# Feed-forward in eleven joint gate-and-up groups of 512 columns, with the product split on VectorE and its tiles 128 bytes further on

## The chip, the core and the metric

One core of a Trainium2 chip runs the whole kernel. The metric is device time in microseconds of one execution. TensorE (PE, with its weight loads as PEld), VectorE (DVE), ScalarE (ACT), GpSimd (POOL) and the DMA queue of SyncE (SP) each work through a list of instructions in order and wait for one another by semaphores.

## The reference

Two layers of a sequence encoder over 256 positions of 2048 features, in float32. Each layer projects x, runs three groups of attention heads, projects back, and ends with a gated feed-forward part, which is what the change touches:

```python
D_FF = (8 * D_MODEL + 3 * 256 - 1) // (3 * 256) * 256      # 5632
...
for li in range(DEPTH):
    ...
    x = layer_norm(DEEPNORM_ALPHA * x + mix, ln1_g[li], ln1_b[li])
    ffn = (jax.nn.silu(x @ w_gate[li]) * (x @ w_up[li])) @ w_down[li]
    x = layer_norm(DEEPNORM_ALPHA * x + ffn, ln2_g[li], ln2_b[li])
```

## The kernel before

**Number format.** Every float32 operand of a large product is cut into a rounded part and a rest (names in `h` and `l`: `whi` and `wlo` for weights, `xth` and `xtl` for the transposed activations, `gth` and `gtl` for the transposed gated product). Each product is three matmuls: hi by hi, lo by hi, hi by lo. The activations (128 features by 128 positions) are the stationary operand, and the weights, up to 512 columns, are the moving one.

**Groups and steps.** `run_groups` takes all products of the kernel as one list of groups. A group has up to 1024 weight columns in two blocks, and `nk` steps of 128 weight rows. In each step and for each half `t` of the positions TensorE does three matmuls on each of the two blocks. So a group of 16 steps is 192 matmuls and a down-projection of 22 steps 264. The four sums (2 halves by 2 blocks) lie in PSUM banks, of which the pool `mm` has five, so the next group starts in the spare bank and then needs the banks of the last one in the order in which they are evacuated. In the last step TensorE finishes the banks one by one, half 0 block 0 first, and each is evacuated as it ends.

**Weights.** `load_pair` brings two steps of weight rows by DMA into one of three `raw` buffers. `convert` makes `whi` on ScalarE (L224) and `wlo` on VectorE (L225), up to four steps ahead, into six buffers.

**Feed-forward.** `ffn_groups` cuts the 5632 inner columns in two halves of 2816. A half is three pairs of groups of 1024, 1024 and 768 columns, first a gate group, then an up group; a group of 768 has two blocks of 384. The gate group's banks leave through a Silu on ScalarE (L1038) into a tile `sil` (four buffers); the up group's banks are multiplied with it on VectorE (L1042). Two down-projection groups (1024 of the 2048 output columns each) end the half. I call the gate and up groups the *ff* stage and the others the *dn* stage; over both layers there are four of each.

**Between the two.** Each product block of 512 columns is handed to a task, `t_g`: sixteen VectorE transposes per block into `gtr` (L406, four at a time), then a rounded copy to `gth` on ScalarE (L285) and the rest to `gtl` on VectorE (L286). Tasks are dealt out between the matmuls in program order by a budget: 0.65 for a step and half at 1024 columns, less for narrower groups. The numbers that tasks yield are this planner's costs. So the pieces of `t_g` stand on ScalarE between the weight conversions, and the Silu of a gate group stands behind whatever pieces were dealt out before it.

**Addresses.** In the built program `raw`, `whi`, `wlo`, `xth` and `xtl` all begin at byte addresses that are 32 modulo 256 within a partition. `gth` begins at 149408 and `gtl` at 171936, which are 160 modulo 256.

Of the kernel before, what the change touches and what calls it, by code (L numbers as in the profile page):

```python
# [10 lines left out]
F32 = mybir.dt.float32  # L11
F32R = mybir.dt.float32r
BF16 = mybir.dt.bfloat16
AF = mybir.ActivationFunctionType
ALU = mybir.AluOpType
AX = mybir.AxisListType

P = 128
SEQ = 256
# [3 lines left out]
KD = D // P  # L23
# [6 lines left out]
OFF_C = OFF_B + 3 * B_W  # L30
OFF_G = OFF_C + 4 * C_W
D_FF = 5632
HALF_FF = D_FF // 2
KH = HALF_FF // P
REL = 513
CHUNK = 64
ALPHA = (2.0 * DEPTH) ** 0.25
# [6 lines left out]
SKEW = 3  # L44
PIECES = ((0, 2), (2, 4), (4, 8), (8, 12), (12, 16))
FAR_AHEAD = 4
EVAC_ACT = (0, 1)
LAST_SKEW = 6
WARM = 9
MM_BUFS = 5  # L50
AUX_BUFS = 3
# [83 lines left out]
class Trunk:  # L135
# [18 lines left out]
    def setup(self):  # L154
# [14 lines left out]
        wps = self.aux()  # L169
        for i in range(WARM):  # L170
            nc.tensor.matmul(wps, warm[:, 0:P], warm, start=True, stop=True)
# [843 lines left out]
    def ffn_groups(self, l):  # L1015
        groups = []
        box = {}
        widths = [1024, 1024, 768]
        for hf in range(2):
            c = 0  # L1020
            for wi, w in enumerate(widths):
                bw = w // 2
                blocks = [(0, bw), (bw, bw)]
                col0 = hf * HALF_FF + c
                kt0 = c // P
                for gu in range(2):
                    def src(k, gu=gu, col0=col0, w=w):
                        return [(self.rows(self.w_up if gu else self.w_gate, l, k * P, col0, w), 0, w)]

                    def start(hf=hf, wi=wi, gu=gu):  # L1030
                        if wi == 0 and gu == 0:
                            self.gt = [self.gpool.tile([P, KH, SEQ], F32R, name=n, tag=n) for n in ("gth", "gtl")]

                    def evac(t, b, bank, gu=gu, bw=bw, kt0=kt0, hf=hf):
                        nc = self.nc
                        if gu == 0:
                            s = self.gpool.tile([P, 512], F32, name="sil", tag="sil", bufs=4)
                            nc.scalar.activation(out=s[:, 0:bw], in_=bank[:, 0:bw], func=AF.Silu)  # L1038
                            box["s", t, b] = s
                        else:  # L1040
                            g = box["s", t, b]
                            nc.vector.tensor_tensor(out=g[:, 0:bw], in0=bank[:, 0:bw], in1=g[:, 0:bw], op=ALU.mult)  # L1042
                            self.tasks.add(self.t_g(g, bw, kt0 + b * bw // P, t, hf))

                    first = hf == 0 and wi == 0 and gu == 0
                    g = dict(name=f"ff{l}.{hf}.{wi}.{gu}", nk=KD, width=w, blocks=blocks, src=src, start=start,
                             evac=evac, lhs=self.hooks_lhs, skew_in=SKEW if first else 1)
                    if first:
                        g["after"] = self.hooks_after
                    groups.append(g)  # L1050
                c += w
            for gi in range(2):
                last = hf == 1 and gi == 1

                def src(k, gi=gi, hf=hf):
                    return [(self.rows(self.w_down, l, hf * HALF_FF + k * P, gi * 1024, 1024), 0, 1024)]

                def lhs(k, t, hf=hf):
                    self.tasks.force(lambda: ("g", hf, k, t) in self.flags)
                    s = slice(t * P, (t + 1) * P)  # L1060
                    return self.gt[0][:, k, s], self.gt[1][:, k, s]

                def start(hf=hf, gi=gi):
                    if hf == 1 and gi == 0:
                        box["stats"] = self.ln_stats()
                        self.ln_load(self.ln2_g, self.ln2_b, l)

                def evac(t, b, bank, hf=hf, gi=gi, last=last):
                    self.res_evac(t, 2 * gi + b, bank, hf == 0, box["stats"] if hf else None)
                    if last and b == 1:  # L1070
                        self.ln_ready(t, box["stats"])
                        if l == DEPTH - 1:
                            for i, (k0, k1) in enumerate(PIECES):
                                self.hooks["apply"](t, i)
                                s = slice(k0 * P, k1 * P)
                                self.nc.sync.dma_start(out=self.out[0, t * P:(t + 1) * P, s], in_=self.xs[t][:, s])

                groups.append(dict(name=f"dn{l}.{hf}.{gi}", nk=KH, width=1024, blocks=[(0, 512), (512, 512)], src=src,
                                   lhs=lhs, start=start, evac=evac))
                if last:  # L1080
                    groups[-1]["skew_out"] = SKEW if l < DEPTH - 1 else LAST_SKEW
                    if l < DEPTH - 1:
                        groups[-1]["mid"] = lambda: self.hooks["need"](0, 0)
        return groups

    def t_g(self, g, bw, kt, t, hf):
        nc = self.nc
        n = bw // P
        gt = self.gpool.tile([P, 4, P], F32, name="gtr", tag="gtr", bufs=2)
        gv = g.rearrange("p (k c) -> p k c", c=P)  # L1090
        yield 1, 0.0
        yield from self.dve_tr(gt, gv, n)
        s = slice(t * P, (t + 1) * P)
        self.split(gt[:, 0:n], self.gt[0][:, kt:kt + n, s], self.gt[1][:, kt:kt + n, s])
        for i in range(n):
            self.flags.add(("g", hf, kt + i, t))
        yield 1, 0.6

    def run(self):
        self.setup()  # L1100
# [31 lines left out]
```

## Time and profile before

| | |
|---|---|
| median of 3 runs | 2394.16 us (2393.36 to 2395.81) |
| the profiled execution, its own time | 2394.55 us |
| its span, first to last instruction | 2392.8 us |
| mean granted TensorE clock | 0.992 |
| TensorE busy | 2350.1 us |
| VectorE busy | 1500.5 us |
| ScalarE busy | 1053.2 us |
| read from HBM | 437.25 MB, 184 GB/s over the span |

The profiled execution's time is 1.75 us more than its span and 0.39 us more than the median. Busy time is the time in which an engine had an instruction in work. Matmuls overlap, so the length of one matmul in the profile is not the time that it costs: what counts is how far apart the starts are, which is the length of a full stretch divided by its number of matmuls.

### The profile page before, as it was taken

Reading aid. Unit: us, or ns where it says so; the run is one execution under the profiler, and the core shown is the slowest. Engines: PE = TensorE matmul, PEld = TensorE weight load, DVE = VectorE, ACT = ScalarE, POOL = GpSimd, SP = SyncE. Lnnn points to the kernel's source line nnn. Section 1 sums busy time; section 2 is a strip of 40 time slices with the busy share of each in tenths; the row PEclk is TensorE's granted clock in tenths of the full one; section 3 lists DMA queues with packets and bytes.
Section 4 is the critical chain, followed back from the end, with each engine's and each line's share of the span. In section 5 each row is a group of like instructions: output and inputs, shape, how many; then the busy total and the mean of one; then the engine's idle time right before and its main releaser. Section 6 shows DMA issues by size and latency. Waiting matters only on the chain.

```text
span 2392.8 us, 28220 instructions
## 1 busy us (share of the span) xinstructions
PE 2350.1 (98%) x10922; PEld 1968.1 (82%) x10922; DVE 1500.5 (63%) x2420; ACT 1053.2 (44%) x1387; POOL 54.9 (2%) x120
## 2 busy tenths in 40 slices
PE   9999999999999999999999999999999999999998
PEld 7887788888888888888788877888888988889886
DVE  5755555758766448667577454557577754487675
ACT  5646454444343344343345554544443343443432
POOL 0001100000000000000000020000000000000000
PEclk9999999999999999999999999999999999999999
DMA  8654455655466555565556544566555565555653
GB/s 279 207 181 158 141 171 199 211 194 194 145 195 206 189 193 183 166 186 193 179 180 206 192 146 140 175 210 211 179 197 151 189 205 190 193 193 150 202 193 106
DMA packets 135414, 441.17 MB, mean 184 GB/s; under 512 B 12560, under 2 KB 19696, under 8 KB 134256
## 3 DMA queue, kind: packets, MB, share of 16 engines
q1 hardware_dynamic: 135136, 439.31, 56.5%
q8 instruction: 85, 1.39, 0.2%
q14 instruction: 49, 0.40, 0.0%
q10 hardware_dynamic: 144, 0.07, 0.0%
HBM read 437.25 MB, written 2.10 MB: 184 GB/s over the span
## 4 chain that ended last, share of the span: by engine, by line
PE 81%; DVE 13%; issue 2%; ACT 1%; DMA 1%; POOL 1%; SPq 0%; POOLq 0%; ACTq 0%
PE mm L272 77%; DVE gtr L406 6%; DVE wlo L225 4%; DMA raw<-w_up 1%; PE aux L295 1%; ACT whi L224 1%; PE aux L542 1%; DVE gtl L286 1%; DVE sil L1042 1%; PE aux L414 1%; DVE x L340 0%; POOL mixc L609 0%; PE aux L715 0%; PE aux L625 0%; DVE bst L319 0%
## 5 line engine op out<-in xcount | busy, mean ns | idle before, releaser
L225 DVE TENSOR_TENSOR wlo<-raw,whi 128x1024 fp32r<-128x1024 f32 (+3 forms) x849 | 991.4, 1173 | 745.2 <-ACT whi L224 739.9
L224 ACT CAST whi<-raw 128x1024 fp32r<-128x1024 f32 (+3 forms) x849 | 849.9, 1010 | 1011.8 <-PE mm L272 979.1
L272 PE MATMUL mm<-whi,xth 128*128 128x512 f32 (+2 forms) x2688 | 831.4, 384 | 23.7 <-ACT sil L1038 23.1
L272 PE MATMUL mm<-wlo,xth 128*128 128x512 f32 (+2 forms) x2688 | 815.9, 379 | 0.0
L272 PE MATMUL mm<-whi,xtl 128*128 128x512 f32 (+2 forms) x2688 | 814.9, 378 | 0.0
L272 PEld LDWEIGHTS mm<-whi,xth 128*128 128x128 f32 x2688 | 491.3, 189 | 107.8 <-ACT sil L1038 26.7
L272 PEld LDWEIGHTS mm<-whi,xtl 128*128 128x128 f32 x2688 | 500.5, 189 | 85.3 <-DVE xtl L286 0.6
L272 PEld LDWEIGHTS mm<-wlo,xth 128*128 128x128 f32 x2688 | 500.8, 189 | 83.8
L406 DVE STREAM_TRANSPOSE gtr<-sil 32x128 f32<-32x128 f32 (+1 forms) x768 | 223.9, 292 | 12.0
L272 PE MATMUL mm<-whi,gth 128*128 128x512 f32 x704 | 226.0, 395 | 0.0
L272 PE MATMUL mm<-whi,gtl 128*128 128x512 f32 x704 | 226.0, 395 | 0.0
L272 PE MATMUL mm<-wlo,gth 128*128 128x512 f32 x704 | 225.9, 395 | 0.0
L272 PEld LDWEIGHTS mm<-whi,gtl 128*128 128x128 f32 x704 | 132.6, 188 | 31.1
L272 PEld LDWEIGHTS mm<-wlo,gth 128*128 128x128 f32 x704 | 132.6, 188 | 31.0
L272 PEld LDWEIGHTS mm<-whi,gth 128*128 128x128 f32 x704 | 132.5, 188 | 30.7
L285 ACT CAST gth<-gtr 128x512 fp32r<-128x512 f32 (+1 forms) x48 | 28.1, 586 | 205.2 <-DVE gtr L406 205.2
L329 POOL TENSOR_SCALAR ve<-mv 128x1 f32<-128x1 f32 x8 | 4.7, 591 | 1809.4 <-DVE mv L327 1809.3
L285 ACT CAST xth<-aux 128x512 fp32r<-128x512 f32 (+1 forms) x58 | 28.9, 512 | 29.5 <-PE aux L295 26.0
L286 DVE TENSOR_TENSOR xtl<-aux,xth 128x512 fp32r<-128x512 f32 (+1 forms) x58 | 33.6, 592 | 5.1 <-ACT xth L285 4.8
L1042 DVE TENSOR_TENSOR sil<-mm,sil 128x512 f32<-128x512 f32 (+1 forms) x48 | 29.1, 643 | 11.8 <-PE mm L272 11.8
L286 DVE TENSOR_TENSOR gtl<-gtr,gth 128x512 fp32r<-128x512 f32 (+1 forms) x48 | 30.7, 639 | 0.1
L340 DVE SCALAR_TENSOR_TENSOR x<-x,rs,lnb 128x512 f32<-128x512 f32 (+1 forms) x40 | 24.7, 639 | 2.8 <-POOL rs L331 2.7
(154 smaller groups left out, 683.9 us busy)
## 6 DMA issues: line engine op xcount, KB each, us to landing
raw<-w_down SPq DMA_DIRECT2D x88, 1024.0 KB, 5.2
raw<-w_in SPq DMA_DIRECT2D x78, 1024.0 KB, 4.9
raw<-w_gate SPq DMA_DIRECT2D x64, 1024.0 KB, 5.0
raw<-w_up SPq DMA_DIRECT2D x64, 1024.0 KB, 5.1
raw<-w_out SPq DMA_DIRECT2D x32, 1024.0 KB, 5.2
raw<-w_in SPq DMA_DIRECT2D x52, 512.0 KB, 3.9
raw<-w_gate SPq DMA_DIRECT2D x32, 768.0 KB, 4.5
raw<-w_up SPq DMA_DIRECT2D x32, 768.0 KB, 4.5
```

The source lines that it names most:

```text
L224: nc.scalar.copy(out=hi[:, s], in_=src[:, s])
L225: nc.vector.tensor_tensor(out=lo[:, s], in0=src[:, s], in1=hi[:, s].bitcast(F32), op=ALU.subtract)
L272: nc.tensor.matmul(banks[t, b][:, 0:w], lt, wt[:, o:o + w], start=(k == 0 and i == 0), stop=(k == nk - 1 and i == 2))
L285: self.nc.scalar.copy(out=hi, in_=ps)
L286: self.nc.vector.tensor_tensor(out=lo, in0=ps, in1=hi.bitcast(F32), op=ALU.subtract)
L295: self.nc.tensor.transpose(out=ps[:, i * P:(i + 1) * P], in_=s, identity=self.ident)
L329: nc.gpsimd.tensor_scalar(out=ve, in0=mv[:, 1:2], scalar1=1.0, scalar2=1e-5, op0=ALU.mult, op1=ALU.add)
L340: nc.vector.scalar_tensor_tensor(out=z, in0=z, scalar=rs, in1=lb[:, s], op0=ALU.mult, op1=ALU.add)
L406: self.nc.vector.transpose(out=out[32 * j:32 * j + 32, 0:n, 32 * i:32 * i + 32], in_=in_[32 * i:32 * i + 32, 0:n, 32 * j:32 * j + 32])
L414: self.nc.tensor.transpose(out=ps[:, i * P:(i + 1) * P], in_=stg[:, i * P:(i + 1) * P], identity=self.ident)
L542: nc.tensor.matmul(ps[:, o:o + SEQ - q0], kt, qt, start=(i == 0), stop=(i == len(pieces) - 1))
L1042: nc.vector.tensor_tensor(out=g[:, 0:bw], in0=bank[:, 0:bw], in1=g[:, 0:bw], op=ALU.mult)
```

## The change

The two halves become 3072 and 2560 columns (`FF_SPLIT = (6, 5)` groups of 512). Each ff group now holds 512 gate columns as block 0 and the same 512 up columns as block 1, so there are no blocks of 384, and a group evacuates a Silu and a product for each half of the positions. The down-projections get 24 and 20 steps. A pair of weight steps arrives as two DMAs of 512 columns where it was one of 1024 or 768. In `t_g` the rounded copy to `gth` moves from ScalarE to VectorE, and the planner's cost of the last piece is 1.2 where it was 0.6. A tile `gpad` of 128 bytes that nothing uses is put ahead of `gth`; with it, and with 24 where there were 22 steps of room, `gth` begins at 149536 and `gtl` at 174112, both 32 modulo 256.

```diff
-HALF_FF = D_FF // 2
-KH = HALF_FF // P
+FF_SPLIT = (6, 5)
+KH = FF_SPLIT[0] * 4
...
+G_PAD = 32
...
-        widths = [1024, 1024, 768]
         for hf in range(2):
...
-                for gu in range(2):
-                    def src(k, gu=gu, col0=col0, w=w):
-                        return [(self.rows(self.w_up if gu else self.w_gate, l, k * P, col0, w), 0, w)]
...
+            blk0 = sum(FF_SPLIT[:hf])
+            for bi in range(FF_SPLIT[hf]):
+                def src(k, col0=(blk0 + bi) * 512):
+                    return [(self.rows(w, l, k * P, col0, 512), i * 512, 512)
+                            for i, w in enumerate((self.w_gate, self.w_up))]
+
+                def start(hf=hf, bi=bi):
+                    if bi == 0:
+                        self.gpool.tile([P, G_PAD], F32, name="gpad")
+                        self.gt = [self.gpool.tile([P, KH, SEQ], F32R, name=n, tag=n) for n in ("gth", "gtl")]
+
+                def evac(t, b, bank, bi=bi, hf=hf):
+                    nc = self.nc
+                    if b == 0:
+                        box["s", t] = self.gpool.tile([P, 512], F32, name="sil", tag="sil", bufs=4)
+                        nc.scalar.activation(out=box["s", t], in_=bank, func=AF.Silu)
+                    else:
+                        g = box["s", t]
+                        nc.vector.tensor_tensor(out=g, in0=bank, in1=g, op=ALU.mult)
+                        self.tasks.add(self.t_g(g, bi * 4, t, hf))
...
-        self.split(gt[:, 0:n], self.gt[0][:, kt:kt + n, s], self.gt[1][:, kt:kt + n, s])
-        for i in range(n):
+        yield 1, 0.0
+        yield from self.dve_tr(gt, g.rearrange("p (k c) -> p k c", c=P), 4)
+        hi, lo = (x[:, kt:kt + 4, t * P:(t + 1) * P] for x in self.gt)
+        nc.vector.tensor_copy(hi, gt)
+        nc.vector.tensor_tensor(out=lo, in0=gt, in1=hi.bitcast(F32), op=ALU.subtract)
+        for i in range(4):
             self.flags.add(("g", hf, kt + i, t))
-        yield 1, 0.6
+        yield 1, 1.2
```

ScalarE before, over the first half's gate group of 768 columns in the first layer, up to its Silu (`whi` with 768 columns is that group's weights and the next one's, `gth` the rounded copy of a product block of the pair of groups before):

```order
L224 CAST whi<-raw 128x768 x9
L285 CAST gth<-gtr 128x4x128
L224 CAST whi<-raw 128x768 x3
L285 CAST gth<-gtr 128x4x128
L224 CAST whi<-raw 128x768 x4
L285 CAST gth<-gtr 128x4x128
L224 CAST whi<-raw 128x768 x3
L285 CAST gth<-gtr 128x4x128
L224 CAST whi<-raw 128x768 x2
L1038 ACTIVATE sil<-mm 128x384 x4
```

ScalarE after the change, from the end of the first ff group's activations through the first Silus (later ff groups repeat the last two rows):

```order
L286 CAST xth<-aux 128x4x128 x2
L225 CAST whi<-raw 128x1024 x4
L1035 ACT_TABLE_LOAD
L1035 ACTIVATE sil<-mm 128x512 x2
L225 CAST whi<-raw 128x1024 x16
```

Nothing that reads `gtr` stands on ScalarE any more, so between two pairs of Silus there are only the sixteen weight conversions of one group.

VectorE before, from the product of the first half's second up group in the first layer into the gate group of 768 columns:

```order
L1042 TENSOR_TENSOR sil<-mm,sil 128x512
L225 TENSOR_TENSOR wlo<-raw,whi 128x768
L1042 TENSOR_TENSOR sil<-mm,sil 128x512 x3
L406 STREAM_TRANSPOSE gtr<-sil 32x4x32 x8
L225 TENSOR_TENSOR wlo<-raw,whi 128x768
L406 STREAM_TRANSPOSE gtr<-sil 32x4x32 x4
L225 TENSOR_TENSOR wlo<-raw,whi 128x768 x2
L406 STREAM_TRANSPOSE gtr<-sil 32x4x32 x4
L225 TENSOR_TENSOR wlo<-raw,whi 128x768
L286 TENSOR_TENSOR gtl<-gtr,gth 128x4x128
```

VectorE after the change, a middle ff group of the first half, from the end of its first task to the products that end it:

```order
L1087 CAST gth<-gtr 128x4x128
L226 TENSOR_TENSOR wlo<-raw,whi 128x1024
L1088 TENSOR_TENSOR gtl<-gtr,gth 128x4x128
L407 STREAM_TRANSPOSE gtr<-sil 32x4x32 x4
L226 TENSOR_TENSOR wlo<-raw,whi 128x1024
L407 STREAM_TRANSPOSE gtr<-sil 32x4x32 x9
L226 TENSOR_TENSOR wlo<-raw,whi 128x1024
L407 STREAM_TRANSPOSE gtr<-sil 32x4x32 x2
L1087 CAST gth<-gtr 128x4x128
L1088 TENSOR_TENSOR gtl<-gtr,gth 128x4x128
L226 TENSOR_TENSOR wlo<-raw,whi 128x1024 x11
L1038 TENSOR_TENSOR sil<-mm,sil 128x512 x2
```

A group now carries two product blocks of tasks where a gate group carried four and an up group none. They are done in the first part of the group, and eleven weight conversions with no task between them stand ahead of the next pair of products.

## Rows read from the trace of the kernel before

**Rows 1.** The page, part 1: busy time, share of the span, instructions.

```profile
PE 2350.1 (98%) x10922; PEld 1968.1 (82%) x10922; DVE 1500.5 (63%) x2420; ACT 1053.2 (44%) x1387; POOL 54.9 (2%) x120
```

**Rows 2.** The view of waits, TensorE: us in total, times, longest us.

```profile
PE mm L272 <- ACT sil L1038: 23.1, 8, 5.4
```

**Rows 3.** Windows over the four ff stages: length, busy by engine, clock, DMA.

```profile
443.40:697.70 254.30, 248.19 (x1183) 215.90 (x1183) 174.59 (x274) 108.51 (x127) 1.72 (x2) 0.99 0.59 191
820.40:1069.90 249.50, 243.73 (x1153) 213.04 (x1152) 158.25 (x245) 102.40 (x116) 0.00 (x0) 0.99 0.58 184
1631.00:1885.40 254.40, 248.36 (x1183) 216.08 (x1183) 174.66 (x274) 108.55 (x127) 1.72 (x2) 0.99 0.59 191
2008.10:2257.80 249.70, 243.80 (x1154) 213.11 (x1153) 158.32 (x245) 102.41 (x116) 0.00 (x0) 0.99 0.58 184
```

**Rows 4.** Windows over the four dn stages: the first, and the sum of all.

```profile
697.70:820.40 122.70, 122.70 (x530) 99.52 (x529) 77.18 (x121) 47.45 (x48) 0.00 (x0) 1.00 0.58 192
...
sum 491.70, PE 491.45 PEld 397.60 DVE 317.78 ACT 184.01 POOL 2.30; mean PE 122.86 PEld 99.40 DVE 79.45 ACT 46.00 POOL 0.58
```

**Rows 5.** Windows over ff groups 1, 3, 4, 5 and 6 of the first stage.

```profile
443.40:491.50 48.10, 47.77 (x224) 38.88 (x224) 37.63 (x48) 23.25 (x28) 1.72 (x2) 1.00 0.67 228
535.20:578.70 43.50, 43.50 (x193) 36.03 (x192) 41.30 (x86) 18.08 (x20) 0.00 (x0) 1.00 0.52 172
578.70:622.90 44.20, 43.81 (x193) 35.96 (x192) 20.36 (x19) 17.88 (x21) 0.00 (x0) 1.00 0.60 192
622.90:656.20 33.30, 33.30 (x193) 33.28 (x192) 31.95 (x76) 12.69 (x17) 0.00 (x0) 1.00 0.47 136
656.20:697.70 41.50, 36.12 (x194) 35.80 (x193) 23.13 (x30) 17.96 (x23) 0.00 (x0) 0.92 0.68 207
```

**Rows 6.** Timeline of ScalarE where group 6 begins: start, length, [idle before <-releaser].

```profile
659.42 0.62 ACT L285 CAST gth<-gtr 128x512 fp32r<-128x512 f32 x1 [5.86 <-DVE gtr L406]
...
661.41 1.62 ACT L1038 ACTIVATE sil<-mm 128x384 f32<-128x384 f32 x4
```

**Rows 7.** Timeline of TensorE at the same place.

```profile
656.23 0.34 PE L272 MATMUL mm<-whi,xth 128*128 128x384 f32 x1
661.95 0.69 PE L272 MATMUL mm<-whi,xth 128*128 128x384 f32 x1 [5.38 <-ACT sil L1038]
```

**Rows 8.** Window over the first matmuls after that wait (clock: third from the end).

```profile
661.90:665.20 3.30, 3.25 (x10) 3.25 (x11) 1.78 (x2) 1.86 (x4) 0.00 (x0) 0.50 0.98 311
```

**Rows 9.** Lines, shapes kept apart: busy, mean ns of one | idle before.

```profile
L225 DVE TENSOR_TENSOR wlo<-raw,whi 128x1024 fp32r<-128x1024 f32 x687 | 837.4, 1224 | 633.2 <-ACT whi L224 629.5
L224 ACT CAST whi<-raw 128x1024 fp32r<-128x1024 f32 x687 | 717.4, 1052 | 860.7 <-PE mm L272 831.8 <-DMA raw<-w_down 8.9 <-DMA raw<-w_up 8.1
L406 DVE STREAM_TRANSPOSE gtr<-sil 32x128 f32<-32x128 f32 x512 | 154.9, 303 | 8.2
L286 DVE TENSOR_TENSOR gtl<-gtr,gth 128x512 fp32r<-128x512 f32 x32 | 21.9, 685 | 0.1
L1042 DVE TENSOR_TENSOR sil<-mm,sil 128x512 f32<-128x512 f32 x32 | 20.6, 685 | 10.6 <-PE mm L272 10.6
L642 DVE TENSOR_SCALAR work<-work,z 128x256 f32<-128x256 f32 x12 | 3.7, 349 | 0.2
L642 DVE TENSOR_SCALAR work<-work,z 128x128 f32<-128x128 f32 x12 | 2.9, 284 | 0.1
```

**Rows 10.** Timelines of ScalarE and TensorE at the end of group 4.

```profile
620.40 0.84 ACT L224 CAST whi<-raw 128x768 fp32r<-128x768 f32 x1 [1.88 <-PE mm L272]
...
622.92 0.51 PE L272 MATMUL mm<-whi,xth 128*128 128x384 f32 x2
```

**Rows 11.** Windows, one input-projection group loaded by two DMAs of 512 columns.

```profile
136.10:181.60 45.50, 45.50 (x211) 37.85 (x210) 19.98 (x18) 22.05 (x29) 0.00 (x0) 1.00 0.56 183
```

More of the change, by code (lines that the diff above doesn't have):

```diff
@@ L1017, in ffn_groups @@
         box = {}
-        widths = [1024, 1024, 768]
         for hf in range(2):
[L1020 to L1025, printed above, removed]
-                for gu in range(2):
-                    def src(k, gu=gu, col0=col0, w=w):
-                        return [(self.rows(self.w_up if gu else self.w_gate, l, k * P, col0, w), 0, w)]
[L1030 to L1051, printed above, removed]
@@ new lines, in ffn_groups @@
+            blk0 = sum(FF_SPLIT[:hf])
[16 more added lines that the diff above has]
+                        self.tasks.add(self.t_g(g, bi * 4, t, hf))
+                first = hf == 0 and bi == 0
+                g = dict(name=f"ff{l}.{hf}.{bi}", nk=KD, width=1024, blocks=[(0, 512), (512, 512)], src=src,
+                         start=start, evac=evac, lhs=self.hooks_lhs, skew_in=SKEW if first else 1)
+                if first:
+                    g["after"] = self.hooks_after
+                groups.append(g)
@@ L1052, in ffn_groups, with src @@
             for gi in range(2):
                 last = hf == 1 and gi == 1
-                def src(k, gi=gi, hf=hf):
-                    return [(self.rows(self.w_down, l, hf * HALF_FF + k * P, gi * 1024, 1024), 0, 1024)]
+                def src(k, gi=gi, blk0=blk0):
+                    return [(self.rows(self.w_down, l, (blk0 * 4 + k) * P, gi * 1024, 1024), 0, 1024)]
                 def lhs(k, t, hf=hf):
@@ L1076, in evac @@
                                 self.nc.sync.dma_start(out=self.out[0, t * P:(t + 1) * P, s], in_=self.xs[t][:, s])
-                groups.append(dict(name=f"dn{l}.{hf}.{gi}", nk=KH, width=1024, blocks=[(0, 512), (512, 512)], src=src,
+                groups.append(dict(name=f"dn{l}.{hf}.{gi}", nk=FF_SPLIT[hf] * 4, width=1024, blocks=[(0, 512), (512, 512)], src=src,
                                    lhs=lhs, start=start, evac=evac))
@@ L1084, in ffn_groups, with t_g @@
         return groups
-    def t_g(self, g, bw, kt, t, hf):
+    def t_g(self, g, kt, t, hf):
         nc = self.nc
-        n = bw // P
         gt = self.gpool.tile([P, 4, P], F32, name="gtr", tag="gtr", bufs=2)
-        gv = g.rearrange("p (k c) -> p k c", c=P)
         yield 1, 0.0
-        yield from self.dve_tr(gt, gv, n)
-        s = slice(t * P, (t + 1) * P)
-        self.split(gt[:, 0:n], self.gt[0][:, kt:kt + n, s], self.gt[1][:, kt:kt + n, s])
-        for i in range(n):
+        yield from self.dve_tr(gt, g.rearrange("p (k c) -> p k c", c=P), 4)
[3 more added lines that the diff above has]
+        for i in range(4):
             self.flags.add(("g", hf, kt + i, t))
-        yield 1, 0.6
+        yield 1, 1.2
     def run(self):
```

## The prediction

> **What bounds the kernel.** I read the page's busy times first: TensorE is busy for 98% of the span [rows 1], so there are two ways to a shorter time, to end its few waits and to make the matmul stream itself denser. The view of waits names the one large wait: eight times, 23.1 us in all, TensorE stood until a Silu on ScalarE had emptied a bank [rows 2]. Then I cut the trace at the group ends. The reader is to see two things in these windows.
>
> First, in the ff stage most groups have the same length, and some do not. A clean group of 1024 columns takes 43.5 us for its 192 matmuls, 226.6 ns from start to start. A clean group of 768 columns takes 33.3 us, 173.4 ns. But the up group of 768 columns takes 41.5 us, and the second up group of 1024 takes 44.2 us [rows 5]. Secondly, the dn stage has no wait at all, and yet its matmuls of the same shape stand further apart: 122.7 us for 528 of them is 232.4 ns [rows 4], 5.8 ns more than in the ff stage.
>
> What happens in the 41.5 us group is in two timelines. ScalarE meets the rounded copy to `gth`, and waits 5.86 us for VectorE's transposes; the four Silus stand behind it in the queue and begin at 661.41 [rows 6]. TensorE starts a matmul at 656.23, and needs a bank that such a Silu frees; the next starts at 661.95 [rows 7]. Right after this wait the granted clock is 0.50, that is 1.2 GHz and not 2.4 [rows 8], so the wait is paid twice. Together 41.5 - 33.3 = 8.2 us. VectorE is late there because this stretch gives it four blocks of tasks beside the conversions of a short group: it is busy for 31.95 of 33.3 us [rows 5].
>
> **The change, part by part.**
>
> *Groups and the Silu wait.* The four ff stages take 254.3 + 249.5 + 254.4 + 249.7 = 1007.9 us [rows 3]. After the change they hold 22 groups of 192 matmuls, all 512 wide. Two of them, each layer's first, also build the transposed activations and wait for them, as now: 48.1 us. The other twenty should be clean: 43.5 us [rows 5]. That is 96.2 + 870 = 966.2 us, a gain of 41.7 us. Of what it consists: the four waits with their slow clock, 4 x 8.2 = 32.8 us; the four short waits at the second up groups, 4 x 0.7 = 2.8 us; and the width. From 173.4 ns at 384 columns and 226.6 ns at 512 a column costs 53.2 / 128 = 0.416 ns and a matmul has a fixed 13.8 ns; 1536 narrow matmuls become 1152 wide ones, so 384 x 13.8 ns = 5.3 us. The rest to 41.7, 0.8 us, is rounding and two waits of some tenths. The Trainium skill, page "TensorE: Matmul & The Clock Gate", section "Wait — 56ns, not 53.3ns?", gives 2.5 ns as the fixed cost of a warm matmul; by it the width would be worth 384 x 2.5 ns = 1.0 us and the total would be 4.3 us less. The trace differs, 13.8 ns, and both widths are measured here.
>
> *Why the wait does not come back elsewhere.* It needed two things: a copy on ScalarE that waits for VectorE, and a VectorE that is late. The copy leaves ScalarE, as the order shows. VectorE's load in a new group is 16 conversions x 1.224 = 19.6, 32 transposes x 0.303 = 9.7, two rests and two products x 0.685 = 2.7, and two of the moved copies. No row shows this copy. Its lower bound comes from a one-input operation: 284 ns at 128 columns and 349 at 256, so 65 ns for each further 128, and 349 + 130 = 0.48 us at 512; its upper bound is the two-input operation of its own shape, 0.685 [rows 9]. I take 0.48, since it has one input. Sum 33.0 to 33.4 us in 43.5. That is less than the 41.3 us which VectorE worked in one 43.5 us group, while TensorE did not wait [rows 5]. So the copy costs nothing; the cover is the 10 us that VectorE has free in each group. If that cover were gone, up to 44 x 0.685 = 30 us would be exposed.
>
> *The evacuation at a group's end* now goes through ScalarE and then VectorE. With the order of the change and the times of [rows 9, 10]: the last weight conversion ahead of the Silus may start 2.5 us before the next group (620.40 against 622.92). It takes 1.05 us, its `wlo` 1.22 us and the first product 0.69 us, so the product ends about 0.5 us into the new group. The Silu it needs is done earlier, in the time of the `wlo`. TensorE asks for that bank after six matmuls, 6 x 0.227 = 1.4 us in. About 0.9 us are left, at every group end. Behind the product on VectorE are the transposes of the new tasks and then conversions that are at least five steps, 13 us, ahead of use. I cost it at nothing.
>
> *Loads.* 1 MB per pair of steps comes in two DMAs of half the row length. An input group that is loaded this way has no wait of TensorE in its window and shows 183 GB/s at a DMA share of 0.56 [rows 11], about the ratio of the 1024-column groups (192 at 0.60 [rows 5]). So 193 GB/s, the need of a 43.5 us group, stays near 0.6. Nothing. The queue's issues are doubled in number, but each conversion runs several steps ahead of use.
>
> *Addresses.* All stationary tiles of the ff stage begin at 32 modulo 256 and their matmuls are 226.6 ns apart; `gth` and `gtl` begin at 160 modulo 256 and theirs are 232.4 ns apart, in the same loop, with the same moving tiles, conversions and clock. VectorE's load doesn't explain it: TensorE holds its 226.6 ns with VectorE busy for 41.30 of 43.5 us [rows 5], while in the dn stage VectorE is busy for 77.18 of 122.7 us only [rows 4]. So the address is what is left, and the change makes it equal. No row varies the address alone, so the bounds are nothing and the full difference, 2112 x 5.8 ns = 12.2 us. I take the full one, since in all else that I can see the two stages are alike.
>
> The sum is 41.7 + 12.2 = 53.9 us. The profiled execution took 2394.55 us, 0.39 us above the median of the runs; 2394.55 - 53.9 = 2340.7, and 2340.3 on the scale of the median. I say 2341.
>
> **The rivals.**
>
> *A. As above*, 2341, with 2337 to 2345 for roundings, and for one more slow-clock stretch or one less in the attention part.
>
> *B. The addresses do nothing* (the change does not do in this part what it says). For it: nothing in the trace varies the address alone, and `gth` also differs from `xth` in its size and in where it lies. Then the dn stage stays at 491.7 us and the time is 2341 + 12 = 2353, with 2349 to 2356. The Trainium skill, page "SBUF — State Buffer", sections "Operand start alignment" and "SBUF: two separate sides", asks only that an operand start at a multiple of its element size, says that rule is not about speed, lists other contention, and says that PE never waits on anyone. By that page the shift would change nothing; the difference of 5.8 ns in the rows has no cause there.
>
> *C. VectorE becomes the wait at the group ends.* Its place is the first product of a group: if VectorE reaches it more than 0.9 us late, TensorE stands before the seventh matmul of the next group. Against it: eleven conversions without a task stand ahead of it, which leave VectorE idle part of the time. One us too late at 22 ends costs 22 us, 2363. Slower than before, by more than 0.2%, it becomes only if each end costs (53.9 + 4.8) / 22 = 2.7 us, so from 3.6 us of lateness on: 2399 and more. A slow clock after such waits would bring this point nearer, as after the 5.4 us wait; the four short waits of now show no such thing (granted clock 1.00 in the 44.2 us group [rows 5]).
>
> *D. The halved DMAs come late* and ScalarE waits for weights in a few groups: some 2 us in each of ten groups, 2361. Against it is [rows 11].
>
> **How the numbers follow.** A 0.76, B 0.14, C 0.06 (a third of it slower than before), D 0.04. The likeliest gives 2341. A alone leaves out more than 2 in 10, so the range goes up through B: 2336 to 2356, which holds 9 in 10 by these chances, less if I have missed a case. About 0.2%, 4.8 us, is what a measurement of this kernel can tell from no change. Only a far C touches it: faster 0.96, same 0.02, slower 0.02.
>
> **What would show each step.** In the profile after: no wait of TensorE for a Silu longer than a few tenths; twenty ff groups of 43.5 us, and two of about 48; a granted clock of 1.00 in the ff stages; VectorE busy 33 us in a group; a dn stage of 24 steps at 288 x 226.6 ns = 65.3 us for each of its two groups, against 66.9 if B holds; and `gth` gone from ScalarE, with a copy of 0.5 to 0.7 us on VectorE. The prediction is wrong if waits of TensorE for the product appear at group ends, or if ScalarE's conversions wait for loads.

## The result, and the profile after

| | before | after |
|---|---|---|
| median, device us | 2393.76 (2391.05 to 2395.81, 4 runs) | 2341.14 (2340.80 to 2342.96, 4 runs) |
| span of the profiled execution | 2392.8 | 2339.4 |
| mean granted TensorE clock | 0.992 | 0.998 |

The ratio is 0.9782, with an interval of 0.9765 to 0.9799: the change takes off 2.2%, 52.6 us by the medians and 53.4 us by the spans. 2341 was predicted. Medians in this document are of undisturbed runs: one of the six runs with the copy back on ScalarE, at 6691.31 us, is left out. Three lines of the page answer to [rows 1]: the span, the busy times and the chain that ended last.

```profile
span 2339.4 us, 27628 instructions
...
PE 2318.4 (99%) x10538; PEld 1905.5 (81%) x10538; DVE 1498.3 (64%) x2360; ACT 1034.5 (44%) x1303; POOL 55.1 (2%) x120
...
PE 96%; DVE 2%; POOL 1%; ACT 1%; DMA 0%; issue 0%; SPq 0%; POOLq 0%
```

VectorE's busy time is the same as before, 1498.3 against 1500.5 us, although it has taken over a copy. So the time was not won by giving VectorE less to do. TensorE has 384 matmuls fewer, 10538 against 10922, by the width of the blocks. Most of the gain came from where the work stands, which the view of waits of the changed kernel shows (TensorE: us in total, times, longest us):

```profile
PE aux L296 <- DVE x L341: 2.2, 6, 0.7
...
PE mm L273 <- ACT whi L225: 0.3, 1, 0.3
```

The Silu of [rows 2], with its eight waits and 23.1 us, is gone from the list. All that the large products (`mm`) still wait for is 0.3 us. Now the stages, as windows of the changed kernel. The columns are the window, its length, the busy time and number of instructions of PE, PEld, DVE, ACT and POOL, the granted clock, the DMA share and GB/s. First come two ff stages and the sum of all four, then the sum of the four dn stages. The last four rows are single groups: the first ff group, an ff group of the middle, and a dn group of 24 steps and one of 20.

```profile
443.20:709.00 265.80, 265.50 (x1183) 218.96 (x1183) 198.04 (x319) 113.73 (x119) 1.72 (x2) 1.00 0.59 200
839.60:1057.20 217.60, 217.60 (x962) 180.18 (x961) 149.77 (x236) 89.76 (x90) 0.00 (x0) 1.00 0.57 193
...
sum 966.80, PE 966.19 PEld 798.27 DVE 695.61 ACT 407.04 POOL 3.43; mean PE 241.55 PEld 199.57 DVE 173.90 ACT 101.76 POOL 0.86
...
sum 479.60, PE 479.26 PEld 396.08 DVE 285.29 ACT 180.34 POOL 2.31; mean PE 119.81 PEld 99.02 DVE 71.32 ACT 45.09 POOL 0.58
...
443.20:491.20 48.00, 47.70 (x223) 38.85 (x223) 37.61 (x48) 23.15 (x28) 1.72 (x2) 1.00 0.67 230
622.00:665.50 43.50, 43.50 (x193) 36.03 (x192) 32.05 (x55) 17.96 (x19) 0.00 (x0) 1.00 0.57 194
709.00:774.30 65.30, 65.30 (x289) 54.05 (x288) 42.30 (x64) 25.48 (x25) 0.00 (x0) 1.00 0.58 193
1057.20:1111.60 54.40, 54.40 (x242) 45.05 (x241) 37.38 (x60) 21.22 (x21) 0.00 (x0) 1.00 0.58 194
```

Against [rows 3] the ff stages went from 1007.9 to 966.8 us, 41.1 less. Against [rows 4] the dn stages went from 491.7 to 479.6, 12.1 less, and their matmuls are 65.3 us / 288 = 226.7 ns apart, as in the ff stage. These two make 53.2 of the 53.4 us. Beside them, one attention group of before had a stretch at the lower clock which this execution of the changed kernel did not have (62.4 us at a mean of 0.97, against 61.5 us at 1.00), 0.9 us, and some tenths elsewhere went the other way.

### The profile page after: what moved, and what is told of

Same layout as the page of the kernel before. It is cut to its first block, busy times and chain, and to the rows that moved or that the text cites. A ratio compares the mean times of both kernels' runs of the same rounds, so it can differ in the third digit from the quotient of the medians.

```text
span 2339.4 us, 27628 instructions
## 1 busy us (share of the span) xinstructions
PE 2318.4 (99%) x10538; PEld 1905.5 (81%) x10538; DVE 1498.3 (64%) x2360; ACT 1034.5 (44%) x1303; POOL 55.1 (2%) x120
## 4 chain that ended last, share of the span: by engine, by line
PE 96%; DVE 2%; POOL 1%; ACT 1%; DMA 0%; issue 0%; SPq 0%; POOLq 0%
PE mm L273 92%; PE aux L296 1%; PE aux L543 1%; PE aux L415 1%; POOL mixc L610 1%; DVE x L341 0%; PE aux L716 0%; PE aux L626 0%; DVE bst L320 0%; DMA raw<-w_in 0%; ACT whi L225 0%; POOL rs L332 0%; POOL ve L330 0%; DVE wlo L226 0%; PE aux L750 0%
## 5 line engine op out<-in xcount | busy, mean ns | idle before, releaser
L226 DVE TENSOR_TENSOR wlo<-raw,whi 128x1024 fp32r<-128x1024 f32 (+2 forms) x817 | 985.8, 1212 | 705.0 <-ACT whi L225 700.9
L225 ACT CAST whi<-raw 128x1024 fp32r<-128x1024 f32 (+2 forms) x817 | 852.6, 1045 | 1172.5 <-PE mm L273 1142.9
L273 PE MATMUL mm<-whi,xth 128*128 128x512 f32 (+1 forms) x2560 | 812.6, 392 | 0.5 <-ACT whi L225 0.3
L273 PE MATMUL mm<-wlo,xth 128*128 128x512 f32 (+1 forms) x2560 | 799.1, 387 | 0.0
L273 PE MATMUL mm<-whi,xtl 128*128 128x512 f32 (+1 forms) x2560 | 798.2, 387 | 0.0
L273 PEld LDWEIGHTS mm<-whi,xtl 128*128 128x128 f32 x2560 | 476.2, 188 | 100.0 <-DVE xtl L287 0.6
L407 DVE STREAM_TRANSPOSE gtr<-sil 32x128 f32<-32x128 f32 x704 | 213.0, 303 | 11.2
L1088 DVE TENSOR_TENSOR gtl<-gtr,gth 128x512 fp32r<-128x512 f32 x44 | 29.9, 681 | 0.7
L1035 ACT ACTIVATE sil<-mm 128x512 f32<-128x512 f32 x44 | 25.9, 594 | 9.9 <-PE mm L273 9.9
L1038 DVE TENSOR_TENSOR sil<-mm,sil 128x512 f32<-128x512 f32 x44 | 28.2, 682 | 1.4 <-ACT sil L1035 1.4
```

The costliest lines, as they stand in the source:

```text
L225: nc.scalar.copy(out=hi[:, s], in_=src[:, s])
L226: nc.vector.tensor_tensor(out=lo[:, s], in0=src[:, s], in1=hi[:, s].bitcast(F32), op=ALU.subtract)
L273: nc.tensor.matmul(banks[t, b][:, 0:w], lt, wt[:, o:o + w], start=(k == 0 and i == 0), stop=(k == nk - 1 and i == 2))
L407: self.nc.vector.transpose(out=out[32 * j:32 * j + 32, 0:n, 32 * i:32 * i + 32], in_=in_[32 * i:32 * i + 32, 0:n, 32 * j:32 * j + 32])
L1035: nc.scalar.activation(out=box["s", t], in_=bank, func=AF.Silu)
L1038: nc.vector.tensor_tensor(out=g, in0=bank, in1=g, op=ALU.mult)
```

## The experiments

All are edits of the changed kernel or of the kernel before. Ratios are against the kernel before, run on the same chip.

### The address alone: take it out, and add it to the kernel before

Out of the changed kernel:

```diff
-                        self.gpool.tile([P, G_PAD], F32, name="gpad")
```

> The change without the 128-byte tile gpad: gth and gtl begin at 160 modulo 256 again, all else as in the changed kernel. Theory (the address sets the spacing of the dn matmuls): ff groups stay at 43.5 us, the dn groups of 24 steps go from 65.3 to 66.9 us and those of 20 steps from 54.4 to 55.8 us, 2112 x 5.8 ns = 12.2 us in all, time 2353. Rival (the regrouping made the dn stage faster, by other step counts or other work beside it): dn stays at 65.3 and 54.4 us, time 2341.

2353.42 us (ratio 0.9836, 0.9822 to 0.9849), 12.3 us more than with the line. A dn group of 24 steps:

```profile
709.30:776.20 66.90, 66.90 (x290) 54.24 (x289) 42.31 (x64) 25.28 (x25) 0.00 (x0) 1.00 0.59 190
```

Into the kernel before, ahead of its `gth`:

```diff
+                            self.gpool.tile([P, 32], F32, name="gpad")
```

> The kernel before with 128 unused bytes ahead of gth and nothing else: gth and gtl at 32 modulo 256. Theory (the address acts by itself, whatever the groups): each dn group of 22 steps goes from 61.3 to 264 x 226.6 ns = 59.8 us, 12.2 us in all, and the Silu waits stay; time 2381. Rival (it needs the new groups): time 2393.

2379.03 us (ratio 0.9946, 0.9932 to 0.9960), 12.5 us less than the kernel before on that chip, 2391.49. A dn group of 22 steps:

```profile
697.60:757.40 59.80, 59.80 (x265) 49.54 (x264) 47.68 (x95) 24.31 (x26) 0.00 (x0) 1.00 0.59 199
```

264 matmuls in 59.8 us are 226.5 ns apart. So the address has its whole price, 12.3 to 12.5 us for 2112 matmuls, with the old groups and with the new ones: it is independent of the regrouping, and adds to it. Rival B, that it does nothing, is out. The Trainium skill, page "SBUF — State Buffer", section "Operand start alignment", gives a rule for where an operand may start, and says of this rule that it is about legality and not about speed. The rule names no cost of an allowed start; here 128 bytes cost 5.8 ns for each matmul, and the measurement decides.

### Which address: the place of a tile, or its distance from the other

In the changed kernel a tile of 128 bytes is put ahead of the weights. That moves `raw`, `whi`, `wlo`, `gth` and `gtl` to 160 modulo 256, and leaves `xth` and `xtl` at 32.

```diff
         self.wp = pool("wp")
+        self.wp.tile([P, 32], F32, name="wpad")
```

> The changed kernel with another 128 bytes put ahead of raw, whi and wlo: these, and gth and gtl behind them, now begin at 160 modulo 256, xth and xtl stay at 32. Theory one (the stationary tile's own address counts): ff stays at 43.5 us a group, dn goes to 66.9 us for 24 steps, time 2353. Theory two (only the distance of the stationary tile from the moving one counts): dn stays at 65.3 us, and all matmuls with xth, 7680 of them, go from 226.6 to 232.4 ns, 44.5 us a... 192 x 232.4 = 44.6 us for an ff group, time about 2341 + 7680 x 5.8 ns = 2385. Theory three (every operand must lie at 32): both slow, about 2397.

2380.51 us (ratio 0.9948, 0.9935 to 0.9962). An ff group, and a dn group of 24 steps:

```profile
634.10:678.90 44.80, 44.80 (x194) 36.04 (x193) 32.13 (x55) 17.90 (x19) 0.00 (x0) 1.00 0.57 189
723.70:789.00 65.30, 65.30 (x290) 54.03 (x289) 42.23 (x64) 25.39 (x25) 0.00 (x0) 1.00 0.58 193
```

The picture is turned round. The dn stage, with both operands at 160, keeps its 226.7 ns; the ff stage, with `xth` at 32 and the weights at 160, now has 44.8 us / 192 = 233.3 ns in the first half (in the second half a group takes 44.6 us, 232.3 ns). So nothing is wrong with the address 160. What counts is how far the stationary tile and the moving one are apart, modulo 256. The kernel loses 39.4 us, and not the 44.5 that the same loss for every one of its large matmuls would give: 192 matmuls at the full loss are 1.1 us, and most of the attention groups, which mix in other matmuls, lose 0.3 to 1.0 us by the starts in the two traces.

`raw` moves together with `whi` and `wlo` here, so the addresses alone do not tell the moving tile from the buffer that it is made from. The end of a kernel does: after its last weight conversion 60 matmuls follow, while ScalarE is idle and nothing reads or writes `raw`. In the changed kernel, and without the pad:

```profile
2312.90:2326.50 13.60, 13.60 (x61) 11.06 (x59) 8.81 (x16) 0.00 (x0) 1.15 (x2) 1.00 0.14 52
2325.00:2339.00 14.00, 14.00 (x61) 11.08 (x60) 8.99 (x16) 0.00 (x0) 1.15 (x2) 1.00 0.15 55
```

13.6 us / 60 is 226.7 ns and 14.0 us / 60 is 233.3 ns: the difference is there without any work on `raw`.

### Other distances

The pad gets another size in each layer, in floats, so that one kernel shows two distances (stationary minus moving, modulo 256 bytes): 32 and 64, then 96 and 160, then 192 and 224.

```diff
-G_PAD = 32
+G_PAD = (40, 48)          # then (56, 8), then (16, 24)
...
-                        self.gpool.tile([P, G_PAD], F32, name="gpad")
+                        self.gpool.tile([P, G_PAD[l]], F32, name="gpad")
```

> The changed kernel with the pad chosen by layer, so that gth and gtl lie 32 bytes modulo 256 past the moving tiles in the first layer and 64 in the second (the change has distance 0, the kernel before 128). Theory (only distance 0 gives the short spacing, any other the long one): dn groups of 24 steps take 66.9 us in both layers, time 2353. Rival (only a distance of 128, half of 256, is bad): 65.3 us in both, time 2341. A third possibility, that some distance is better than 0, would show as less than 65.3 us; matmul spacing could at best fall toward 512 columns at the slope of 0.416 ns, 213 ns, 61.3 us.

> As the run with distances 32 and 64, with 96 in the first layer and 160 in the second. Theory (distance 0 alone is good): dn groups of 24 steps 66.9 us in both layers, time 2353. Rival (128 alone is bad): 65.3 us, time 2341. In between, if the spacing grows with the distance to the nearest multiple of 256: 66 to 66.9 us, 2347 to 2353.

> As the run with distances 32 and 64, with 192 in the first layer and 224 in the second. Theory (distance 0 alone is good): dn groups of 24 steps 66.9 us in both layers, time 2353. Rival (128 alone is bad): 65.3 us, time 2341. If the sign of the distance matters, these differ from the run with 32 and 64.

2356.26, 2356.05 and 2350.07 us, one run each. The dn groups of 24 steps of the third kernel, distance 192 and then 224:

```profile
709.20:775.20 66.00, 66.00 (x290) 54.13 (x289) 42.38 (x64) 25.32 (x25) 0.00 (x0) 1.00 0.58 193
1871.60:1938.80 67.20, 67.20 (x289) 53.98 (x288) 42.33 (x64) 25.29 (x25) 0.00 (x0) 1.00 0.57 188
```

| distance, bytes | 0 | 32 | 64 | 96 | 128 | 160 | 192 | 224 |
|---|---|---|---|---|---|---|---|---|
| dn group of 24 steps, us | 65.3 | 67.2 | 67.2 | 67.5 | 66.9 | 67.2 | 66.0 | 67.2 |

Zero is the best of the eight, and 192 comes next. The order of the others follows no rule that I can name, and their differences of 0.3 us are no larger than what one distance shows: at 128 the ff groups of the run with moved weights had 232.3 ns in one half and 233.3 ns in the other, which is 0.3 us in 288 matmuls.

### The regrouping alone, and the copy back on ScalarE

The changed kernel with the rounded copy on ScalarE again:

```diff
-        nc.vector.tensor_copy(hi, gt)
-        nc.vector.tensor_tensor(out=lo, in0=gt, in1=hi.bitcast(F32), op=ALU.subtract)
+        self.split(gt, hi, lo)
```

> The changed kernel with the rounded copy to gth put back on ScalarE; groups, widths and addresses as in the change. Theory (the wait needs both a copy on ScalarE and a VectorE that is late): VectorE has 33 us of work in a 43.5 us group and is not late, so ScalarE waits for transposes in the middle of a group but never with a Silu behind it; no wait of TensorE for a Silu, time 2341, within 1 us. Rival (the copy on ScalarE makes the wait by itself): waits of 0.7 us or more come back at most of the 20 group ends, time 2355 and more.

2341.41 us (ratio 0.9786, 0.9772 to 0.9799): the same as the changed kernel. The trace is that of one more run of the same kernel.

> The changed kernel with the rounded copy on ScalarE once more, for its trace. Theory: ScalarE waits for the transposes at its two copies per group, some microseconds each, and TensorE never waits for a Silu; ff groups of 43.5 us, time 2341.

2342.70 us. TensorE's view of waits has no line of `mm` at all. ScalarE's has this one:

```profile
ACT gth L286 <- DVE gtr L407: 165.6, 44, 5.8
```

ScalarE's timeline in a middle ff group of the same kernel (start, length, idle before and its releaser):

```profile
684.26 0.62 ACT L286 CAST gth<-gtr 128x512 fp32r<-128x512 f32 x1 [5.84 <-DVE gtr L407]
684.78 2.95 ACT L225 CAST whi<-raw 128x1024 fp32r<-128x1024 f32 x3
```

Here is the wait of [rows 6] again, 5.84 us against 5.86. ScalarE waits for the transposes 44 times, 165.6 us in all, and it costs TensorE nothing. Behind it stand weight conversions, which are steps ahead of their use, and no Silu.

The changed kernel with both taken back, the copy and the pad, so that the regrouping is left alone:

> The eleven joint groups alone: the rounded copy on ScalarE and gth at 160 modulo 256, both as before the change. Theory (the regrouping makes the whole gain of the ff stage, the moved copy nothing): ff groups of 43.5 us, dn groups of 66.9 and 55.8 us, time 2353.5, that is 39.7 us less than before. Rival (the moved copy has a share): ff groups over 44 us, time over 2356.

2354.42 us (ratio 0.9844, 0.9830 to 0.9857). A middle ff group, and a dn group of 24 steps:

```profile
622.00:665.50 43.50, 43.50 (x193) 36.04 (x192) 31.47 (x53) 18.77 (x21) 0.00 (x0) 1.00 0.60 195
709.10:776.00 66.90, 66.90 (x290) 54.24 (x288) 41.75 (x62) 26.12 (x27) 0.00 (x0) 1.00 0.58 190
```

On that chip the regrouping takes off 2391.49 - 2354.42 = 37.1 us by itself; the kernel before was 2.3 us faster there than its median in the table above, and against that median it is 39.3. And 2354.42 against the 2353.42 us of the kernel without the pad says once more that in the new groups the engine of the copy is worth about 1 us at most.

### The copy alone, in the kernel before

```diff
-        self.split(gt[:, 0:n], self.gt[0][:, kt:kt + n, s], self.gt[1][:, kt:kt + n, s])
+        hi, lo = (x[:, kt:kt + n, s] for x in self.gt)
+        nc.vector.tensor_copy(hi, gt[:, 0:n])
+        nc.vector.tensor_tensor(out=lo, in0=gt[:, 0:n], in1=hi.bitcast(F32), op=ALU.subtract)
```

> The kernel before with one edit: the rounded copy to gth goes to VectorE. Groups of 1024 and 768 columns, addresses as before. Theory (the Silus were late only because they stood behind a copy that waited for VectorE): the four waits of 5.4 us, the slow clock behind them and the four short waits go, 32.8 + 2.8 = 35.6 us, time about 2358. Rival (a late VectorE is enough: the Silus write into tiles that still have to be transposed, and VectorE gets 4 x 0.4 us more work in its fullest stretch): the 41.5 us groups stay at 40 us or more, time 2385 to 2394.

2377.49 us (ratio 0.9937, 0.9925 to 0.9950). That is neither nothing nor the 35.6 us of the eight waits: by the spans it is 2392.8 - 2377.1 = 15.7. Its waits, of TensorE and of ScalarE:

```profile
PE mm L272 <- ACT sil L1038: 13.2, 8, 1.9
...
ACT whi L224 <- DMA raw<-w_up: 71.6, 27, 4.5
```

Its windows over the second up group and the narrow up group of the first half:

```profile
580.00:625.40 45.40, 43.89 (x194) 35.98 (x194) 21.15 (x20) 18.68 (x21) 0.00 (x0) 1.00 0.62 197
658.70:695.60 36.90, 35.15 (x194) 34.84 (x193) 23.84 (x33) 16.82 (x21) 0.00 (x0) 0.95 0.70 224
```

The timeline of ScalarE where the narrow up group begins:

```profile
659.49 0.83 ACT L224 CAST whi<-raw 128x768 fp32r<-128x768 f32 x1 [3.94 <-DMA raw<-w_up]
660.23 1.25 ACT L1038 ACTIVATE sil<-mm 128x384 f32<-128x384 f32 x3
```

The narrow up group went from 41.5 to 36.9 us, and the second one got longer, from 44.2 to 45.4 [rows 5]. The Silus no longer stand behind a copy that waits for VectorE's transposes, and they still come late: now a conversion stands in front of the first three that waits 3.94 us for its weights. (The fourth waits 1.02 us for transposes of VectorE, which read the tile that it writes into.) The mean of 0.95 holds a stretch at 0.50 behind TensorE's wait, from 662.2 to 665.5. In the second layer TensorE waits 1.8 us at the same place and the clock stays at 1.00, so the group is shorter:

```profile
1839.20:1874.60 35.40, 33.62 (x194) 33.30 (x193) 23.68 (x33) 16.53 (x21) 0.00 (x0) 1.00 0.75 235
```

Why is a load late? `raw` is free only when VectorE has made `wlo` from it, and VectorE is late. If that is so, a fourth `raw` buffer should end it. To make room, the converted tiles go from six buffers to five, and the skew of the last group goes from 6 to 4. On top of the edit above:

```diff
-H_BUFS = 6
-RAW_BUFS = 3
+H_BUFS = 5
+RAW_BUFS = 4
...
-LAST_SKEW = 6
+LAST_SKEW = 4
```

> The kernel before with the rounded copy on VectorE, as in the run of that name, and a fourth raw buffer, which is paid for with a fifth instead of a sixth buffer of whi and wlo (and 4 skewed last steps for 6). Theory (there a late VectorE still holds up the Silu because it frees the raw buffers late, so that loads start late and ScalarE waits for them in front of the Silu): the waits at the 384-column up groups go from 2 us to some tenths, these groups from 35.4 to 36.9 us to 33.3 to 34 us, those of the second up groups from 45.3 to 43.5 to 44 us. Rival (the Silu waits for its own tile, which VectorE has not transposed yet, or for VectorE in another way): the waits stay at 1.5 to 2 us. The attention part may lose by the missing buffers, so it is the ff windows that count, not the time.

2375.18 us (ratio 0.9930, 0.9917 to 0.9944). The largest wait of TensorE:

```profile
PE mm L272 <- DVE wlo L225: 4.9, 8, 0.9
```

The same two up groups:

```profile
579.50:623.00 43.50, 43.50 (x193) 36.05 (x192) 20.96 (x20) 16.62 (x18) 0.00 (x0) 1.00 0.62 201
...
657.00:692.10 35.10, 33.86 (x194) 33.22 (x194) 22.86 (x31) 14.70 (x18) 0.00 (x0) 1.00 0.77 251
```

No wait of TensorE for a Silu is left, ScalarE waits for no `w_up` load, and the second up group has its 43.5 us back. So the late load was the link, for all that the second up group had lost. In front of the narrow up group, where VectorE is crowded, the wait moved to the last thing that VectorE makes, `wlo`: this group takes 35.1 us in both layers and not 33.3, so without the slow clock, against the 35.4 us above, the buffer is worth 0.3 us there. The fourth Silu waits longer for VectorE's transposes than before, and TensorE does not wait for it:

```profile
ACT sil L1038 <- DVE gtr L406: 11.9, 4, 3.0
```

The kernel as a whole is only 2.3 us faster than with the copy alone, since other groups got longer: the narrow gate group takes 34.0 us and not 33.3. Which of the three changed numbers does that was not tried.

### VectorE later, in the changed kernel

Each transpose of `t_g` is done twice, at the same planner's cost, which adds 9.7 us of VectorE's work to an ff group:

```diff
-                self.nc.vector.transpose(out=out[32 * j:32 * j + 32, 0:n, 32 * i:32 * i + 32],
-                                         in_=in_[32 * i:32 * i + 32, 0:n, 32 * j:32 * j + 32])
+                for _ in range(2):
+                    self.nc.vector.transpose(out=out[32 * j:32 * j + 32, 0:n, 32 * i:32 * i + 32],
+                                             in_=in_[32 * i:32 * i + 32, 0:n, 32 * j:32 * j + 32])
```

> The changed kernel with every VectorE transpose of the product done twice in place, at the same planner's cost: 32 more of 0.303 us in an ff group, so VectorE has 42.3 us of work in 43.5 us. It prices the cover of the moved copy. Theory (the average load decides, as 41.3 of 43.5 us did no harm before): no new wait of TensorE, time 2341. Rival (it is the place that decides: the tasks are dealt out over the first 20 of 32 budget steps, there VectorE would have 1.4 times what fits): conversions of the middle of the group come about 2 us late, 2 us in each of 20 groups and more with a slow clock behind, time 2380 to 2440.

2376.36 us (ratio 0.9927, 0.9911 to 0.9944), 35.2 us more than the changed kernel. Its waits:

```profile
PE mm L273 <- ACT sil L1036: 14.1, 17, 1.5
PE mm L273 <- DVE wlo L226: 8.4, 18, 0.5
...
ACT whi L225 <- DMA raw<-w_up: 223.3, 60, 6.9
```

A middle ff group:

```profile
581.70:627.10 45.40, 44.08 (x193) 35.83 (x192) 41.26 (x86) 17.27 (x19) 0.00 (x0) 1.00 0.54 184
```

VectorE is busy for 41.26 of 45.4 us, and TensorE waits. Before, one 43.5 us group had 41.30 us of VectorE's work and no wait [rows 5]. The same busy time costs 1.9 us here and nothing there. What makes the difference was not separated: here every group is crowded and is followed by another, and there the next group had no tasks, and lost 0.7 us. The first crowded group of a stage points the same way without settling it. Of these four, one loses nothing with VectorE busy for 39.77 us, and the others take 44.1, 44.7 and 45.2 us:

```profile
893.20:936.70 43.50, 43.50 (x193) 36.04 (x192) 39.77 (x85) 16.13 (x17) 0.00 (x0) 1.00 0.53 175
```

## Why the prediction was right, point by point

The total came nearer than its parts: 2341.14 us against 2341 is in part luck. The sum was 53.9 us and the windows of the two stages give 53.2, 2341 was rounded up from 2340.3 on the scale of the median, and the 0.9 us of lower clock in the attention part was allowed for in the range but in no term of the sum.

**Groups and the Silu wait.** Predicted 41.7 us, measured 41.1. Twenty groups of 43.5 and two of about 48 were predicted; 20 x 43.5 + 2 x 48.0 = 966.0, and the four windows give 966.8. The regrouping alone gives the ff part, since its middle group has 43.5 us with the copy on either engine. The division of the 41.7 into waits (32.8 + 2.8) and width (5.3) was not tried by itself: no run here changed only the width, or only the dealing out of the tasks.

**Why the wait does not come back.** This step gave the right answer by a reason that is half wrong: "It needed two things: a copy on ScalarE that waits for VectorE, and a VectorE that is late." The copy is not needed. With the copy gone from ScalarE but the old groups kept, eight Silu waits of up to 1.9 us remain, and in the changed kernel with doubled transposes they come back, both without such a copy. The second half stands: in the new groups, where VectorE is done with its tasks well before the group's end, the copy on ScalarE waits 165.6 us and costs nothing. In these runs a stall took a late VectorE and a Silu that stands soon behind something it holds up. Two such things reached TensorE: the copy, and a `raw` buffer that is freed late, whose next load is then late. The wait of a Silu for the transposes of its own tile, up to 3.0 us with four `raw` buffers, did not. The regrouping ends both. By the orders and the traces it does so by dealing two blocks of tasks to every group early on, where four fell to one group and none to the next; no run shows that apart from the rest of the regrouping.

**The moved copy.** I bounded it by 0.48 and 0.685 us and took 0.48. It took 0.402 us, below my lower bound, by the lines of the changed kernel (busy, mean ns, idle before):

```profile
L1087 DVE CAST gth<-gtr 128x512 fp32r<-128x512 f32 x44 | 17.7, 402 | 0.8
L1088 DVE TENSOR_TENSOR gtl<-gtr,gth 128x512 fp32r<-128x512 f32 x44 | 29.9, 681 | 0.7
```

The slope of another one-input operation was not a lower bound. VectorE was busy for 32.05 us in a middle group, where my sum had 33.0. The copy cost nothing, as I said (2341.14 against 2341.41 us), but "the cover is the 10 us that VectorE has free in each group" is too generous: 9.7 us more work cost 35.2 us over the kernel. The cover is smaller than the idle time, and I did not measure where it ends.

**The evacuation at a group's end.** I had 0.5 us into the new group for the end of the first product, and 0.9 us left. Timelines of the changed kernel at the end of that group, ScalarE, VectorE, TensorE:

```profile
662.99 1.05 ACT L225 CAST whi<-raw 128x1024 fp32r<-128x1024 f32 x1 [1.67 <-PE mm L273]
663.95 0.59 ACT L1035 ACTIVATE sil<-mm 128x512 f32<-128x512 f32 x1
...
664.08 1.22 DVE L226 TENSOR_TENSOR wlo<-raw,whi 128x1024 fp32r<-128x1024 f32 x1 [1.50 <-ACT whi L225]
665.22 1.28 DVE L1038 TENSOR_TENSOR sil<-mm,sil 128x512 f32<-128x512 f32 x2
...
665.51 0.62 PE L273 MATMUL mm<-whi,xth 128*128 128x512 f32 x2
...
666.87 0.62 PE L273 MATMUL mm<-whi,xth 128*128 128x512 f32 x2
```

The new group starts at 665.51. The two products take 1.28 us from 665.22, so the first ends at about 665.9, 0.4 us in, and TensorE starts the matmul that needs its bank at 666.87, without a wait. That leaves 1.0 us. Rival C did not occur.

**Loads.** "Stays near 0.6" was right: DMA share 0.57 and 194 GB/s in the middle group. ScalarE waited once in the ff and dn stages for a load, 1.8 us for `w_up` in the first ff group, and TensorE did not wait for it. So the sign that I had named for rival D appeared once, and the rival's cost did not.

**Addresses.** Predicted 12.2 us, measured 12.1 in the windows, and 12.3 and 12.5 by the edit alone. My reason, that all else is alike and so the address is what is left, held. What I had not seen is that it is the distance between two tiles.

## What to carry to other kernels

Look for what stands behind a wait in its engine's queue: a wait of 5.8 us is free in front of work that is steps ahead, and dear in front of the evacuation that the next group needs. When tasks are dealt out between matmuls, spread them evenly and end them well before the evacuation, since a late engine also frees load buffers late, and the stall then shows up under another name. Where two loops of the same matmul have different spacings, compare the start addresses of the stationary and the moving tile before looking for anything deeper.

## What the runs showed of the hardware

The spacing of 128x512 float32r matmuls depended on the distance between the stationary and the moving tile, modulo 256 bytes: 65.3 us for 288 of them at a distance of 0, which is 226.7 ns, 66.0 (229.2) at 192, 66.9 (232.3) at 128, and 67.2 to 67.5 (233.3 to 234.4) at the other five steps of 32 bytes. At 128 other groups showed 233.3 ns as well. The cause is open: the runs show the dependence, also with ScalarE idle (13.6 against 14.0 us for 60 matmuls), and no part of the chip that it comes from. The second thing is the clock: TensorE's stop of 5.4 us was followed by a stretch at 0.50 [rows 8]. With the copy moved, the narrow up groups of the first layer have a mean of 0.95 after waits of 1.7 and 1.8 us, and those of the second layer 1.00 after waits of 1.8 and 1.9 us; the groups with doubled transposes, with waits of at most 1.5 us, show 1.00. So the length of the stop alone did not decide here whether the clock fell.
